# Half-size products in both MLP matmuls, with the gated result through DRAM

## The chip, the cores and the metric

The kernel runs on one core of a Trainium2 chip. The metric is the device time of one execution in microseconds (us). The core has five engines with a queue of their own each: TensorE (PE in the rows; PEld is its weight load), VectorE (DVE), ScalarE (ACT), GpSimd (POOL) and SyncE (SP), which issues all transfers (DMA) here. An engine takes its instructions strictly in the order of its queue and waits at each until its operands are there.

## The reference

Two layers of an encoder, S = 1024 rows, width 1024, in float32. A layer is four groups of attention heads on a common input projection, an output projection and a gated MLP. The change touches the MLP:

```python
        x = x + mix @ w_out[l]

        h = _rmsnorm(x, norm2_g[l])
        u = _dwconv3(h @ w_up[l], conv_w[l], conv_b[l])
        gate, val = u[..., :D_FF], u[..., D_FF:]
        x = x + (jax.nn.silu(gate) * val) @ w_down[l]
```

D_FF is 2816, so w_up is 1024 x 5632 and w_down 2816 x 1024. `_dwconv3` is a convolution of width 3 along the rows, for each column by itself, with a bias.

## The kernel before

A matmul in float32 is made of three in a faster type: `split` stores an operand as a high part (a copy into float32r by ScalarE) and a low part (the operand minus the high part, by VectorE or GpSimd, L130), and `mm` (L141) is called for the three pairs in `PASSES`, high with high and high with low both ways. Each call has a 128x128 weight and 512 moving columns in the MLP.

After attention the second norm turns x, in 8 tiles of 128 rows, into `h2T`, transposed and split: `h2T0` has rows 0 to 511 of the sequence, `h2T1` rows 512 to 1023. This is the tail of the attention stage (`out`, `norm`); its casts of `mT` (the transposed attention result, L1067) and `h2T` (L171) run on ScalarE, the matmuls are `od`, the transposes `ntp`. Its order is written out by hand; the generator `mlp` is advanced inside it and yields after each of its first steps.

The MLP goes over j = 0 to 21 (NFF = 22), 128 of the 2816 columns at a time. `up(j)` loads two 512 KB weights `rawu` (gate part, then value part), splits them (`wu`, high by ScalarE, low by GpSimd), and makes two products `u` of 128 x 1024 in PSUM, 8 chunks of the inner 1024 by 3 passes by 2 halves = 48 matmuls each. `conv` reads u from PSUM (L937 on ScalarE, L938 and L939 on VectorE) and writes `c` in SBUF; `gate` applies silu (L944), multiplies on GpSimd (L945) and splits the result into `gt`. `down(j-1)` then multiplies the previous `gt` with 128 rows of w_down (`rawd`, `wd`): 8 row tiles by 3 passes by 2 halves = 48 matmuls `d`, and VectorE adds each 128 x 1024 result to `xacc`, the running x (L968). So up(j) and down(j-1) alternate, and only down(21) stands alone. j = 0 begins already in the tail of the norm, with the half h2T0. A scheduler places the instructions of the MLP in the queues by its own estimate of when they can run. The pool `raw` has two buffers, `wu`, `wd`, `gt`, `u` and `d` two each.

The order of SP around the start of the MLP matters below: the four small, scattered loads `cw` (conv weights and bias, L917 and L918) are issued ahead of the weights of j = 1 (L922).

## Time and profile before

| | |
|---|---|
| median of 3 runs | 3197.47 us (3197.13 to 3202.42) |
| the profiled execution | 3201.03 us, its span 3199.2 us |
| TensorE busy | 3031.2 us, 95% of the span, 16800 matmuls |
| VectorE, ScalarE, GpSimd busy | 2021.4, 1424.2, 920.5 us (63%, 45%, 29%) |
| granted TensorE clock, mean | 0.987 of full speed |
| MLP of layer 0, from the first u to the last d | 867 to 1605 us |
| MLP of layer 1 | to the end of the span |

The profile is one execution. A row of a group names line, engine, operation and tiles, then the busy time, the mean of one in ns, the idle time of the engine before it and what ended that. A row of a stretch gives for each engine its busy time in that stretch and the count of its instructions. The granted clock is 1.00 at the higher of the two levels (2.4 GHz) and 0.50 at the lower (1.2 GHz).

### The profile page before, as it was taken

The page shows a single profiled execution, that of the slowest core. Times are in us where ns is not written, and L with a number is a line of the kernel's source. Part 1 is how long each engine was busy: PE and PEld are TensorE (multiplying, and loading weights), DVE is VectorE, ACT ScalarE, POOL GpSimd, SP SyncE. Part 2 cuts the span into 40 slices and gives each one's busy share as a digit, 9 for nine tenths or more (in the row PEclk, how much of TensorE's full clock was granted, in tenths as well). Part 3 has the DMA queues.
Part 4 walks back from the last instruction along what each step waited for, and adds up shares of the span by engine and source line. Part 5 has one row for each costly group of instructions (what it writes and reads, how often), then busy time and mean ns, then how long its engine had stood idle before and what let it go on. Part 6 is the DMA issues. An engine that isn't in the chain of part 4 may idle for free. (4 is left out here: it accounts for less than half of the span.)

```text
span 3199.2 us, 44078 instructions
## 1 busy us (share of the span) xinstructions
PE 3031.2 (95%) x16800; PEld 2601.1 (81%) x16800; DVE 2021.4 (63%) x3304; ACT 1424.2 (45%) x2653; POOL 920.5 (29%) x780
## 2 busy tenths in 40 slices
PE   7988899899999999999989899998999999999999
PEld 5978888788888888888769788887888888888887
DVE  6778877777734444444576788777776444444445
ACT  5557765766622222222144577657665222222211
POOL 2265310320232323323222663103201333232221
PEclk9999999999999999999999899999999999999999
DMA  4342241321311111111133322414212111111111
GB/s 140 113 105 67 63 132 40 85 71 31 49 60 46 47 47 47 52 47 50 37 126 108 101 65 66 132 40 91 65 36 39 60 47 53 47 53 40 53 47 66
DMA packets 276867, 212.99 MB, mean 67 GB/s; under 512 B 197168, under 2 KB 242608, under 8 KB 276656
## 3 DMA queue, kind: packets, MB, share of 16 engines
q1 hardware_dynamic: 276656, 210.18, 22.4%
q8 instruction: 132, 2.16, 0.3%
q14 instruction: 79, 0.65, 0.1%
HBM read 157.70 MB, written 41.94 MB: 62 GB/s over the span
## 5 line engine op out<-in xcount | busy, mean ns | idle before, releaser
L141 PE MATMUL u<-h2T,wu 128*128 128x512 f32 x4224 | 1013.7, 392 | 0.0
L141 PEld LDWEIGHTS u<-h2T,wu 128*128 128x128 f32 x4224 | 792.3, 188 | 179.9
L968 DVE TENSOR_TENSOR xacc<-xacc,d 128x1024 f32<-128x1024 f32 x352 | 424.7, 1217 | 460.0 <-PE d L141 459.6
L141 PE MATMUL d<-wd,gt 128*128 128x512 f32 x2112 | 525.7, 392 | 4.1 <-DVE xacc L968 4.1
L141 PE MATMUL pj<-w,hT 128*128 128x256 f32 (+2 forms) x3072 | 494.1, 315 | 24.3 <-ACT w L134 12.9
L141 PEld LDWEIGHTS pj<-w,hT 128*128 128x128 f32 x3072 | 443.0, 196 | 51.5 <-ACT w L134 14.3
L141 PEld LDWEIGHTS d<-wd,gt 128*128 128x128 f32 x2112 | 394.7, 188 | 97.0 <-DVE xacc L968 10.6
L130 POOL TENSOR_TENSOR wu<-rawu,wu 128x1024 fp32r<-128x1024 f32 x88 | 212.3, 2414 | 655.9 <-ACT wu L134 655.9
L487 ACT CAST PT<-pt 128x512 fp32r<-128x512 f32 x448 | 261.6, 584 | 183.7 <-PE pt L145 175.4
L937 ACT ACTIVATE c<-u,cw 128x1024 f32<-128x1024 f32 x88 | 106.3, 1208 | 527.9 <-PE u L141 527.8
L488 DVE TENSOR_TENSOR PT<-pt,PT 128x512 fp32r<-128x512 f32 x448 | 305.1, 686 | 49.6 <-ACT PT L487 47.0
L145 PE MATMUL pt<-cst,P 128*128 128x128 f32 x1792 | 278.5, 279 | 55.2 <-DVE PT L488 49.4
L938 DVE SCALAR_TENSOR_TENSOR c<-u,cw,c 128x1023 f32<-128x1023 f32 x88 | 112.9, 1283 | 297.1 <-ACT c L937 297.0
L145 PEld LDWEIGHTS pt<-cst,P 128*128 128x128 f32 x1792 | 209.7, 142 | 88.7 <-issue 37.8
L141 PEld LDWEIGHTS ot<-PT,v 128*128 128x128 f32 x1664 | 255.7, 192 | 32.1
L141 PE MATMUL ot<-PT,v 128*128 128x256 f32 x1664 | 270.9, 285 | 0.0
L141 PE MATMUL S<-k,q 96*128 96x512 f32 (+2 forms) x512 | 209.6, 435 | 16.9 <-DVE nmb L653 14.9
L141 PE MATMUL od<-wo,mT 128*128 128x512 f32 x768 | 199.9, 399 | 0.9 <-DVE mT L1017 0.7
L130 POOL TENSOR_TENSOR wd<-rawd,wd 128x1024 fp32r<-128x1024 f32 x44 | 105.5, 2398 | 289.4 <-ACT wd L134 289.4
L653 DVE CUSTOM_DVE_ANT_0 P<-S,toep 128x1024 f32<-128x1024 f32 x128 | 155.6, 1219 | 27.3 <-PE pt L145 23.2
L134 ACT CAST gt<-c 128x1024 fp32r<-128x1024 f32 x44 | 46.3, 1053 | 283.5 <-POOL c L945 283.5
L545 DVE TENSOR_REDUCE nm<-S 128x1 f32<-128x1024 f32 x128 | 156.0, 1219 | 19.2 <-PE S L141 18.6
(200 smaller groups left out, 3898.0 us busy)
## 6 DMA issues: line engine op xcount, KB each, us to landing
rawu<-in_w_up_dram SPq DMA_DIRECT2D x88, 512.0 KB, 3.2
rawd<-in_w_down_dram SPq DMA_DIRECT2D x44, 512.0 KB, 3.2
rawi<-in_w_in_dram SPq DMA_DIRECT2D x20, 512.0 KB, 4.0
rawo<-in_w_out_dram SPq DMA_DIRECT2D x16, 512.0 KB, 3.3
sC<-cqk SPq DMA_DIRECT2D x16, 384.0 KB, 2.5
ld<-sB SPq DMA_DIRECT2D x24, 256.0 KB, 3.6
sD<-pe SPq DMA_DIRECT2D x48, 128.0 KB, 1.7
ld<-sC SPq DMA_DIRECT2D x16, 384.0 KB, 3.5
```

What stands on the lines that cost most here:

```text
L130: eng.tensor_tensor(dst[1], src, dst[0].bitcast(F32), op=ALU.subtract)
L134: self.nc.scalar.copy(dst, src)
L141: self.nc.tensor.matmul(out, l, r, start=start, stop=stop)
L145: self.nc.tensor.transpose(out, in_, self.ident[:p, :p])
L487: nc.scalar.copy(PT[:, 0, :], pt)
L488: nc.vector.tensor_tensor(PT[:, 1, :], pt, PT[:, 0, :].bitcast(F32), op=ALU.subtract)
L545: nc.vector.tensor_reduce(nm, Ps["S", i], axis=AX.X, op=ALU.max, negate=True)
L653: nc.vector.tensor_tensor_reduce(out=P, in0=Ps["S", i, s], in1=self.toep[:, o:o + S], scale=-slope, scalar=-NEG, op0=ALU.add, op1=ALU.min, ...
L937: nc.scalar.activation(c, u, AF.Identity, scale=cw[:, 1, jj:jj + 1], bias=cw[:, 3, jj:jj + 1])
L938: nc.vector.scalar_tensor_tensor(c[:, 1:], u[:, :S - 1], cw[:, 0, jj:jj + 1], c[:, 1:], op0=ALU.mult, op1=ALU.add)
L968: nc.vector.tensor_tensor(xacc[:, t, :], xacc[:, t, :], d, op=ALU.add)
```

## The change

Both products are cut two by two (rows and columns of each operand in halves), and the four quarters of the result come from seven half-size products instead of eight, with sums and differences of quarters made beforehand.

In the up product, for j = 1 to 21 (j = 0 stays as it was), the left quarters are the halves of the inner 1024 of gate weight and value weight, `a11`, `a12`, `a21`, `a22`, four sums of which are built in place in the raw buffers by GpSimd (`G`) and VectorE (`V`). The right operands `T1`, `T2`, `T3`, `T4` are built once a layer from `h2T`, which means joining high and low part, four differences and a new split. `T3` overwrites a quarter of h2T1. Each of the seven products has 4 chunks x 3 passes = 12 matmuls into a PSUM tile `X` (8 buffers), and ScalarE, VectorE and GpSimd combine them into `u`, which now lies in SBUF, as `conv` then reads it. The gated result `v` is stored in a DRAM tensor `gd` (11.5 MB per layer) instead of being split.

The down product is a stage of its own after the last gate: `down` loads all 22 tiles of `gd` back (`gg`, 512 KB each) and then runs seven products, each over 11 chunks, where chunk c joins rows c and c + 11 of the 22. A chunk loads one or two 256 KB pieces of w_down (`rawd`, 6 buffers `rw`), adds two of them on GpSimd where two terms are listed in `DOWN`, adds g terms on VectorE, splits both, and issues 4 x 3 = 12 matmuls. The low part of w_down is made by GpSimd for odd c and by VectorE for even c. VectorE adds each finished product to one to two quarters of `xacc`.

The pools move too: `mp` stands on the other side of SBUF, the pool of the attention's output stage is closed earlier and a new one (`oq`) is opened with the last w_out loads, so that these loads and those of j = 0's weights come earlier. `wu` is now cut in halves of the inner dimension, with six buffers.

```diff
@@ -908,10 +908,13 @@
-    def mlp(self, l, xacc, h2T, mp):
+    def mlp(self, l, h2T, mp, gd):
...
         def load(jj):
             raw = self.raw.tile([128, KC, 128], F32, tag="raw", name="rawu")
             nc.sync.dma_start(raw, a["w_up"][l, jj])
-            w = mp.tile([128, 2, KC, 128], F32R, tag="wu", name="wu", bufs=2)
-            self.split((w[:, 0], w[:, 1]), raw, "act", "pool")
-            return w
-
-        def product(u, w, halves):
+            return raw
+
+        def operand():
+            return mp.tile([128, 2, 4, 128], F32R, tag="wu", name="wu", bufs=6)
+
...
+        def gate(j, us):
+            g, v = (conv(jj, u) for jj, u in zip((j, NFF + j), us))
+            nc.scalar.activation(g, g, AF.Silu)
+            G.tensor_tensor(v, v, g, op=ALU.mult)
+            nc.sync.dma_start(gd[j * 128:(j + 1) * 128, :], v)
+
+
+        ws = []
+        for jj in (0, NFF):
+            raw, w = load(jj), []
+            for h in range(2):
+                w.append(operand())
+                self.split((w[h][:, 0], w[h][:, 1]), raw[:, 4 * h:4 * h + 4, :], "act", "pool")
+            ws.append(w)
+        yield
...
-        def gate(us, gt):
-            g, v = us
-            nc.scalar.activation(g, g, AF.Silu)
-            nc.gpsimd.tensor_tensor(v, v, g, op=ALU.mult)
-            self.split((gt[:, 0], gt[:, 1]), v, "act", "dve")
...
-        def down(j, gt):
-            raw = self.raw.tile([128, DM], F32, tag="raw", name="rawd")
-            nc.sync.dma_start(raw, a["w_down"][l, j * 128:(j + 1) * 128, :])
-            w = mp.tile([128, 2, DM], F32R, tag="wd", name="wd", bufs=2)
-            self.split((w[:, 0], w[:, 1]), raw, "act", "pool")
-            for t in range(NT):
-                d = pm.tile([128, DM], F32, tag="d", name="d", bufs=2)
-                for i, (x, y) in enumerate(PASSES):
-                    for n in range(2):
-                        self.mm(d[:, n * 512:(n + 1) * 512], gt[:, x, t * 128:(t + 1) * 128],
-                                w[:, y, n * 512:(n + 1) * 512], i == 0, i == 2)
-                nc.vector.tensor_tensor(xacc[:, t, :], xacc[:, t, :], d, op=ALU.add)
-
...
-            down(j - 1, prev)
+            product(u, w, 1)
+        gate(0, uu)
+        tp, pm = yield
+        T1, T2, T4 = (tp.tile([128, 2, 4, 512], F32R, tag=f"T{i}", name=f"T{i}") for i in (1, 2, 4))
+        T3 = h2T[1][:, :, 0:4, :]
+        B11, B21, B22 = h2T[0][:, :, 0:4, :], h2T[0][:, :, 4:8, :], h2T[1][:, :, 4:8, :]
+
+        for k in range(4):
+            f = [mp.tile([128, 2, 512], F32, tag="u", name="bf", bufs=3) for _ in range(2)]
+            b11, b12, b22, b21 = f[0][:, 0], f[0][:, 1], f[1][:, 0], f[1][:, 1]
+            for d, t in ((b11, B11), (b12, T3), (b22, B22), (b21, B21)):
+                V.tensor_tensor(d, t[:, 0, k, :].bitcast(F32), t[:, 1, k, :].bitcast(F32), op=ALU.add)
+            V.tensor_tensor(b11, b12, b11, op=ALU.subtract)
+            G.tensor_tensor(b12, b22, b12, op=ALU.subtract)
+            V.tensor_tensor(b22, b22, b11, op=ALU.subtract)
+            G.tensor_tensor(b21, b21, b22, op=ALU.subtract)
+            for t, d, eng in ((T1, b11, "dve"), (T2, b22, "dve"), (T3, b12, "pool"), (T4, b21, "pool")):
+                self.split((t[:, 0, k, :], t[:, 1, k, :]), d, "act", eng)
...
+        def prod(w, t):
+            ps = pm.tile([128, 512], F32, tag="X", name="X", bufs=8)
+            i = 0
+            for k in range(4):
+                for x, y in PASSES:
+                    self.mm(ps, w[:, x, k, :], t[:, y, k, :], i == 0, i == 11)
+                    i += 1
+            return ps
+
+        for j in range(1, NFF):
+            rg, rv = load(j), load(NFF + j)
...
+            w11 = op(a11, "pool")
+            G.tensor_tensor(a21, a21, a22, op=ALU.add)
+            s1 = op(a21, "dve")
+            V.tensor_tensor(a11, a21, a11, op=ALU.subtract)
+            s2 = op(a11, "dve")
+            w12 = op(a12, "pool")
+            w22 = op(a22, "pool")
+            G.tensor_tensor(a22, a22, a11, op=ALU.subtract)
+            s3 = op(a22, "pool")
+            V.tensor_tensor(a12, a12, a11, op=ALU.subtract)
+            s4 = op(a12, "dve")
+
...
+            nc.scalar.copy(g[:, lo], prod(w11, B11))
+            nc.scalar.copy(t5, prod(s1, T1))
+            V.tensor_tensor(t2, g[:, lo], prod(s2, T2), op=ALU.add)
+            G.tensor_tensor(g[:, hi], t2, t5, op=ALU.add)
+            V.tensor_tensor(g[:, lo], g[:, lo], prod(w12, B21), op=ALU.add)
+            V.tensor_tensor(v[:, hi], t2, prod(s3, T3), op=ALU.add)
+            V.tensor_tensor(g[:, hi], g[:, hi], prod(s4, B22), op=ALU.add)
+            V.tensor_tensor(v[:, lo], v[:, hi], prod(w22, T4), op=ALU.add)
+            G.tensor_tensor(v[:, hi], v[:, hi], t5, op=ALU.add)
+            gate(j, (g, v))
...
+    DOWN = (
+        (((0, 0, 1),), ((0, 1, 1), (1, 1, -1)), ((0, 1, 1), (1, 1, 1))),
+        (((0, 0, 1), (0, 1, 1)), ((1, 1, 1),), ((0, 0, -1), (0, 1, 1))),
...
+    def down(self, l, xacc, gp, sp, pm, gd):
...
+        for j in range(NFF):
+            gs.append(gp.tile([128, S], F32, tag=f"g{j}", name="gg"))
+            nc.sync.dma_start(gs[-1], gd[j * 128:(j + 1) * 128, :])
+
+        def operand(tag, terms, add, low):
+            w = sp.tile([128, 2, 512], F32R, tag=tag, name=tag, bufs=3)
+            t = terms[0][0]
+            if len(terms) > 1:
+                u, sign = terms[1]
+                d = sp.tile([128, 512], F32, tag="sum", name="sum", bufs=3) if tag == "ga" else t
+                add.tensor_tensor(d, t, u, op=ALU.add if sign > 0 else ALU.subtract)
+                t = d
+            self.split((w[:, 0], w[:, 1]), t, "act", low)
+            return w
+        for As, Bs, Cs in self.DOWN:
+            ds = [pm.tile([128, 512], F32, tag="d", name="d", bufs=8) for _ in range(4)]
+            for c in range(NH):
+                ta = [(gs[c + NH * k][:, i * 512:(i + 1) * 512], sign) for i, k, sign in As]
+                tb = []
+                for k, j, sign in Bs:
+                    raw = sp.tile([128, 512], F32, tag="rw", name="rawd", bufs=6)
+                    r0 = (c + NH * k) * 128
+                    nc.sync.dma_start(raw, a["w_down"][l, r0:r0 + 128, j * 512:(j + 1) * 512])
+                    tb.append((raw, sign))
+                w = operand("ga", ta, V, "dve")
+                m = operand("wd", tb, P, "pool" if c % 2 else "dve")
+                for t in range(4):
+                    for i, (x, y) in enumerate(PASSES):
+                        self.mm(ds[t], w[:, x, t * 128:(t + 1) * 128], m[:, y, :], c == 0 and i == 0, c == NH - 1 and i == 2)
+            for i, j, sign in Cs:
+                for t in range(4):
+                    xs = xacc[:, 4 * i + t, j * 512:(j + 1) * 512]
+                    V.tensor_tensor(xs, xs, ds[t], op=ALU.add if sign > 0 else ALU.subtract)
...
-                    st["mlp"] = self.mlp(l, st["x"], h2, me.enter_context(self.pool(f"mp{l}", side=gs)))
+                    st["mlp"] = self.mlp(l, h2, me.enter_context(self.pool(f"mp{l}", side=at)), gd)
...
-            try:
-                st["mlp"].send(me.enter_context(self.pool(f"pm{l}", space=PS)))
-            except StopIteration:
-                pass
+            o2.close()
+            with ExitStack() as te:
+                try:
+                    st["mlp"].send((te.enter_context(self.pool(f"T{l}", side=gs)), te.enter_context(self.pool(f"pm{l}", space=PS))))
...
             halves.close()
-            oe.close()
+            with ExitStack() as te:
+                self.down(l, xacc, te.enter_context(self.pool(f"G{l}", side=gs)), te.enter_context(self.pool(f"dw{l}", side=gs)),
+                          te.enter_context(self.pool(f"pd{l}", space=PS)), gd)
```

ScalarE in the tail of layer 0's second norm, before the change. `rawu_9862` and `rawu_9867` are the weights of j = 0:

```order
L134 CAST wu_9864<-rawu_9862 128x1024
L134 CAST wu_9869<-rawu_9867 128x1024
L1067 CAST mT_9877<-mtp_9872 128x256
L171 CAST h2T0_8975<-ntp_9885 128x4x128
L155 ACTIVATE od2_9830,nss_9844<-xacc_4940 128x1024
L171 CAST h2T0_8975<-ntp_9892 128x4x128
L1067 CAST mT_9880<-mtp_9872 128x256
L1067 CAST mT_9923<-mtp_9918 128x256
```

Only j = 0's weights are cast here. The same place on ScalarE after the change (`rawu_9867` and `rawu_9875` belong to j = 0, `rawu_10290` to j = 1):

```order
L134 CAST wu_9877<-rawu_9875 128x512
L134 CAST wu_9880<-rawu_9875 128x512
L1159 CAST mT_9888<-mtp_9883 128x256
L171 CAST h2T0_9311<-ntp_9896 128x4x128
L155 ACTIVATE od2_9835,nss_9849<-xacc_4941 128x1024
L171 CAST h2T0_9311<-ntp_9903 128x4x128
L1159 CAST mT_9891<-mtp_9883 128x256
L134 CAST wu_10294<-rawu_10290 128x512
L1159 CAST mT_9934<-mtp_9929 128x256
L171 CAST h2T0_9311<-ntp_9942 128x4x128
```

A cast of j = 1's gate weight now stands between two casts of mT, ahead of the rest of the norm.

SP at the end of layer 0's MLP, before; `rawq` and `rawk` are weights of the next layer:

```order
L959 DMA rawd<-in_w_down_dram 128x1024
L922 DMA rawu<-in_w_up_dram 128x1024 x2
L959 DMA rawd<-in_w_down_dram 128x1024
L922 DMA rawu<-in_w_up_dram 128x1024 x2
L959 DMA rawd<-in_w_down_dram 128x1024 x2
L1149 DMA rawq<-in_c_wqb_dram 128x2x384
L1153 DMA rawk<-in_c_wkvb_dram 128x512
```

Loads of both weights alternate up to the end. SP at the end of the up product of layer 0, after the change:

```order
L925 DMA rawu<-in_w_up_dram 128x1024 x2
L942 DMA gd_1774<-c 128x1024
L925 DMA rawu<-in_w_up_dram 128x1024 x2
L942 DMA gd_1774<-c 128x1024
L1241 DMA rawq<-in_c_wqb_dram 128x2x384
L1245 DMA rawk<-in_c_wkvb_dram 128x512
L942 DMA gd_1774<-c 128x1024 x2
L1049 DMA gg<-gd_1774 128x1024 x22
L1069 DMA rawd<-in_w_down_dram 128x512 x106
```

The w_down loads, which alternated with the w_up loads, now all stand behind the last two stores of gated results and the 22 loads of g.

GpSimd in the middle of the MLP, for one j, before:

```order
L945 TENSOR_TENSOR c<-c 128x1024
L130 TENSOR_TENSOR wu<-rawu,wu 128x1024
L130 TENSOR_TENSOR wd<-rawd,wd 128x1024
L130 TENSOR_TENSOR wu<-rawu,wu 128x1024
L945 TENSOR_TENSOR c<-c 128x1024
```

That is a product and three splits for one j. GpSimd for one j of the up product, after the change (`t_11041` and `t_11042` are the tiles t2 and t5):

```order
L1021 TENSOR_TENSOR u<-t_11041,t_11042 128x512
L130 TENSOR_TENSOR wu<-rawu,wu 128x512 x2
L1010 TENSOR_TENSOR rawu<-rawu 128x512
L130 TENSOR_TENSOR wu<-rawu,wu 128x512
L1026 TENSOR_TENSOR u<-u,t_11042 128x512
L1004 TENSOR_TENSOR rawu<-rawu 128x512
L130 TENSOR_TENSOR wu<-rawu,wu 128x512
L941 TENSOR_TENSOR c<-c 128x1024
```

Three splits and a product of 128x1024 became eight instructions on 128x512 and the product, and the last two of the eight (L1004 and L130 ahead of L941) belong to a later j.

## Rows read from the trace of the kernel before

**Rows 1.** the page: busy us and share; TensorE's granted clock in 40 slices.

```profile
PE 3031.2 (95%) x16800; PEld 2601.1 (81%) x16800; DVE 2021.4 (63%) x3304; ACT 1424.2 (45%) x2653; POOL 920.5 (29%) x780
...
PEclk9999999999999999999999899999999999999999
```

**Rows 2.** a stretch: busy us by engine (PE, PEld, DVE, ACT, POOL); clock, DMA, GB/s.

```profile
915.00:1580.00 665.00, 665.00 (x2883) 541.12 (x2882) 309.88 (x260) 148.75 (x140) 189.99 (x79) 1.00 0.14 47
```

**Rows 3.** costliest groups of the page, the two MLP products: busy us, mean ns.

```profile
L141 PE MATMUL u<-h2T,wu 128*128 128x512 f32 x4224 | 1013.7, 392 | 0.0
...
L141 PE MATMUL d<-wd,gt 128*128 128x512 f32 x2112 | 525.7, 392 | 4.1 <-DVE xacc L968 4.1
```

**Rows 4.** the stretch at the end of layer 0, columns as in rows 2.

```profile
1583.00:1606.00 23.00, 21.20 (x84) 14.96 (x84) 19.63 (x18) 2.87 (x4) 2.39 (x1) 1.00 0.34 140
```

**Rows 5.** timeline of TensorE between the layers: start, us, instruction, [idle before it].

```profile
1612.05 1.30 PE L145 MATMUL ntp<-cst,nx 128*128 128x128 f32 x5 [6.69 <-DVE nr L117]
```

**Rows 6.** timeline of SP (issues) in the tail of layer 0's second norm.

```profile
849.43 8.01 SPq L917 DMA_DIRECT2D cw<-in_conv_w_dram  x3
857.48 3.31 SPq L918 DMA_DIRECT2D cw<-in_conv_b_dram  x1
860.83 3.63 SPq L922 DMA_DIRECT2D rawu<-in_w_up_dram  x1
```

**Rows 7.** tile rawu, 855 to 870 us: time from issue to landing.

```profile
DMA to landing us min/median/max: 5.1/6.4/7.6
```

**Rows 8.** timeline of ScalarE in the tail of the norm.

```profile
853.69 0.38 ACT L1067 CAST mT<-mtp 128x256 fp32r<-128x256 f32 x1
```

**Rows 9.** tile wo, its splits: ns min/median/max, first and last start, shape.

```profile
L130 POOL TENSOR_TENSOR wo<-rawo,wo x32: 720/747/931, 412.7 to 2395.3; 128x256 fp32r<-128x256 f32 x32
L130 DVE TENSOR_TENSOR wo<-rawo,wo x32: 407/620/969, 413.6 to 2397.0; 128x256 fp32r<-128x256 f32 x32
```

**Rows 10.** line 968, one operand in PSUM, columns as in rows 9.

```profile
L968 DVE TENSOR_TENSOR xacc<-xacc,d x352: 1208/1220/1222, 917.2 to 3194.4; 128x1024 f32<-128x1024 f32 x176
```

**Rows 11.** groups of GpSimd by shape: busy us, mean ns, idle before.

```profile
L130 POOL TENSOR_TENSOR wu<-rawu,wu 128x1024 fp32r<-128x1024 f32 x88 | 212.3, 2414 | 655.9 <-ACT wu L134 655.9
...
L945 POOL TENSOR_TENSOR c<-c 128x1024 f32<-128x1024 f32 x44 | 105.5, 2397 | 73.0 <-DVE c L939 71.6 <-issue 1.4
...
L130 POOL TENSOR_TENSOR w<-rawi,w 128x512 fp32r<-128x512 f32 x32 | 40.7, 1290 | 1.3 <-ACT w L134 1.1
```

**Rows 12.** groups of VectorE by shape, columns as in rows 11.

```profile
L938 DVE SCALAR_TENSOR_TENSOR c<-u,cw,c 128x1023 f32<-128x1023 f32 x88 | 112.9, 1283 | 297.1 <-ACT c L937 297.0
...
L130 DVE TENSOR_TENSOR gt<-c,gt 128x1024 fp32r<-128x1024 f32 x44 | 53.7, 1220 | 13.3 <-ACT gt L134 13.3
...
L130 DVE TENSOR_TENSOR w<-raw,w 128x512 fp32r<-128x512 f32 x16 | 10.7, 688 | 4.3 <-ACT w L134 4.3
```

**Rows 13.** timelines of GpSimd and VectorE in the third wo split.

```profile
712.25 3.18 POOL L130 TENSOR_TENSOR wo<-rawo,wo 128x256 fp32r<-128x256 f32 x4 [6.68 <-ACT wo L134]
...
713.05 1.79 DVE L130 TENSOR_TENSOR wo<-rawo,wo 128x256 fp32r<-128x256 f32 x2
```

**Rows 14.** DMA issues over the whole span: KB each, us to landing.

```profile
rawu<-in_w_up_dram SPq DMA_DIRECT2D x88, 512.0 KB, 3.2
...
ld<-sB SPq DMA_DIRECT2D x24, 256.0 KB, 3.6
...
mx<-mix SPq DMA_DIRECT2D x22, 256.0 KB, 2.6
```

**Rows 15.** groups of ScalarE by shape, columns as in rows 11.

```profile
L937 ACT ACTIVATE c<-u,cw 128x1024 f32<-128x1024 f32 x88 | 106.3, 1208 | 527.9 <-PE u L141 527.8
...
L944 ACT ACTIVATE c<-c 128x1024 f32<-128x1024 f32 x44 | 46.7, 1062 | 117.3 <-DVE c L939 117.3
```

**Rows 16.** a stretch of layer 1 with many loads, columns as in rows 2.

```profile
2008.00:2022.00 14.00, 10.23 (x43) 8.51 (x43) 9.82 (x19) 6.65 (x13) 1.13 (x2) 0.63 1.02 395
```

**Rows 17.** the restart after the gap between the layers, columns as in rows 2.

```profile
1617.00:1622.00 5.00, 4.89 (x11) 3.48 (x12) 4.67 (x10) 3.44 (x8) 1.34 (x1) 0.50 0.53 169
```

More of the change, by code (lines that the diff above doesn't have):

```diff
@@ L1185, in run @@
             h2, wo = [], []
[L1186 removed]
+            halves, me, o2 = ExitStack(), ExitStack(), ExitStack()
+            gd = dp.tile([FF, S], F32, tag=f"gd{l}", name=f"gd{l}")
             def norm2(t, r):
```

63 lines of the change are left out of this document (31 added, 32 removed), and 5 rows, old and new, of the table DOWN.

## The prediction

> **What bounds the kernel now.** I read the page first, then the engines by stretch, then the places where TensorE waits. TensorE is busy for 95% of the span at full clock in nearly every slice [rows 1]. In the gated MLP it is the only limit: between 915 and 1580 us it is busy for all of 665.00 us and issues 2883 matmuls, so one 128x512 matmul costs 665.00/2883 = 0.2307 us [rows 2], while VectorE works for 47% of that stretch and GpSimd for 29%. The two MLP products hold 4224 and 2112 matmuls [rows 3], 6336 x 0.2307 = 1462 us of the 3201. Fewer matmuls there shorten the kernel one for one, as long as the other engines and the transfers stay beside them. That condition is what has to be examined.
>
> **What the change removes.** Each j from 1 to 21 of the up product takes 7 x 12 = 84 matmuls in place of 96, so 252 fewer per layer. The down product takes 7 x 11 x 12 = 924 in place of 1056, so 132 fewer. 384 x 0.2307 = 88.6 us per layer, **177 us** in all. The last 84 down matmuls of layer 0 begin at 1583 and are done at 1612.05 - 6.69 = 1605.4, 22.4 us against 84 x 0.2307 = 19.4, since there are two accumulators that VectorE must drain [rows 4, 5]; with eight half-size ones that goes: **6 us** in two layers. Between the layers TensorE idles 6.69 us for the next norm [rows 5]; rows 0 to 511 of x are now final before the last product, so I take **5 us** for this. Removed: 188 us, 3201 - 188 = 3013.
>
> **What it adds at the start of the MLP.** In the new order ScalarE casts j=1's first weight between two casts of mT. That weight's DMA stands on SP behind the four cw loads, whose issue takes 8.01 and 3.31 us, so it is issued at 860.83 and lands 5.1 to 7.6 us later [rows 6, 7], at some 868.4. ScalarE would come there at 854.1, just after the cast of 853.69 [rows 8]; it waits 14 us, and the norm of the second half, the transposes and the first u products all queue behind it. With a restart at half clock I take **16.5 us** a layer (8 to 20), 33 in all.
>
> **What VectorE and GpSimd do to each other.** The change puts many 128x512 sums and differences of two SBUF operands on both. Where they meet in the trace they exclude one another: in the wo split a GpSimd 128x256 takes 720 ns alone and up to 931, a VectorE one 407 alone and up to 969 [rows 9]. VectorE's xacc adds, which have one operand in PSUM, stay at 1208 to 1222 ns in all 352 cases, whatever GpSimd does [rows 10]. The price of a turn: from 512 to 1024 columns GpSimd grows by 2.414 - 1.290 = 1.124 us and VectorE by 1.220 - 0.688 = 0.532 [rows 11, 12]; these parts cannot overlap. Four GpSimd and two VectorE rows of 256 columns stand in 3.18 us [rows 13]: 4 x 0.562 + 2 x 0.266 = 2.78, the rest is 0.067 a turn. So a 128x512 turn costs 1.19 on GpSimd and 0.60 on VectorE. No row shows so dense a mixture for long; the sum of turns is my value, the two ends are no exclusion at all and full durations.
>
> The Trainium skill states the rule ("SBUF — State Buffer", Who interferes with whom): a VectorE instruction with two SBUF inputs and a GpSimd one that reads SBUF exclude each other, and the loser is blocked for the whole instruction. The trace agrees that they do, but 3.18 us for that group is less than 4 x 0.720 + 2 x 0.407 = 3.69, so whole durations are too dear by its rows.
>
> - *The T operands*, once a layer: 32 VectorE turns and 16 GpSimd turns, 32 x 0.60 + 16 x 1.19 = 38.2 us, with the first gate's product (2.3) and what is left of j=1's operands (4) 44.5 us after the second half of h2T. The cover is 48 u0 matmuls (11.1) and the seven products of j=1 (19.4), 30.5 us. Lost: 14, and as the first sums read h2T0 alone I take **13** a layer, 26 in all. Without exclusion VectorE alone needs 32 x 0.688 and j=0's four conv rows at 1.28, 27 us, and the last T come some 5 late; by full durations 32 x 0.688 + 16 x 1.29 + 2.4 + 4.5 = 49.5, 19 late [rows 11, 12].
> - *The up product in its steady state.* Per j, GpSimd has eight 128x512 and one 128x1024 (10 x 1.124 + 9 x 0.067 = 11.84 us). VectorE has five 128x512 and four conv rows of 128x1023, whose u now lies in SBUF (13 x 0.532 + 9 x 0.067 = 7.52). Together 19.36, against 84 x 0.2307 = 19.38 on TensorE: exactly level. Operands are made about 8 us before they are needed and eight PSUM tiles hold the results, so single collisions are hidden; but any moment in which neither has work (the casts between, the raw load of 3.2 us for the next j [rows 14]) is then late. I take 0.4 us per j, 42 x 0.4 = **17 us**. Ends: 0, and by full durations 8 x 1.29 + 2.40 + 5 x 0.688 + 4 x 1.28 = 21.28, so 1.9 per j, 80 us [rows 11, 12].
> - *The down product.* Two chunks are 24 matmuls, 5.54 us. Three of the seven products have two terms on both sides: GpSimd 3 turns (3.57), VectorE 5 (3.0), 6.57 us, over by 1.03 on 16.5 pairs of chunks. Two products have two w_down terms and one g term; their turns sum to 5.37, but a loop stands there: GpSimd's low part frees a buffer, SP loads 256 KB into it, GpSimd adds (1.29) and makes the next low part (1.29), one such round for two chunks. A 256 KB transfer lands after 2.6 to 3.6 us [rows 14]; 2.6 + 0.1 + 2.58 with one VectorE turn of 0.6 between is 5.9, over by 0.4 on 11 pairs. 16.5 x 1.03 + 11 x 0.4 = 21.4 a layer, **43 us**. Ends: 5 (landing 2.6, no collision) and 88 (full durations, landing 3.6).
>
> **What it adds between the products.** Formerly down(j-1) ran beside up(j), now it begins when the last gate is done. After the last up matmul: VectorE's add 0.69 and conv 1.28, ScalarE's silu 1.06 and conv 1.21, VectorE 2 x 1.28, GpSimd's product 2.40 [rows 11, 12, 15], about 10 us with the semaphores. SP issues the stores of j=20 and 21, then 22 loads of g, and only then w_down, in that order on one queue. With all DMA engines busy the core moves 395 GB/s [rows 16], so 512 KB take 1.33 us; 25 such portions are 33 us, and with some 2 us of latency the first pair of w_down lands 45 us after the last up matmul. Sum and split are another 2 us, and TensorE restarts at half clock, as it ran for 1617 to 1622 after the gap between the layers [rows 17]: 2.5 us. **49 us** a layer, 98 in all (90 to 110). Nothing covers it, since TensorE has no other work there. The rest (the stores of g, smaller and more w_down loads, four late adds at the very end) lies beside other work; its cover is a DMA share of 0.14 [rows 2].
>
> **The sum.** 3013 + 33 + 26 + 17 + 43 + 98 = 3230 us for the profiled execution. The profiled run of before, 3201.0, is 3.6 us over its median of 3197.5, so the forecast is **3226 us**, 0.9% slower: the transitions (157 us) and the shared path (60) eat the 188.
>
> **Rivals.** (1) *Faster:* VectorE and GpSimd are kept apart by their queues. For: in the old MLP they hardly meet, and the operands' lead is 8 us. Against: 19.36 of 19.38 us leaves nothing to place. Then T loses 5 a layer, up 0, down 5: 3013 + 33 + 10 + 5 + 98 = 3159, median 3155. It decides once the three terms, 86 in my sum, fall under 57. (2) *Much faster:* the gap between the products is also short, because transfers of g overlap or the first w_down pair overtakes them. At 20 us a gap instead of 49 this takes 58 more off, about 3100. Against: the one queue. (3) *Clearly slower:* each of the two engines holds the other off for its whole instruction: 38 for T, 80 for up, 88 for down, 3013 + 33 + 38 + 80 + 88 + 98 = 3350, median 3346. Against: the 3.18 us group. It decides once a turn costs its whole duration. (This is what the Trainium skill's section named above gives for this kernel.) (4) *No change:* terms between mine and rival 1 that meet the 188.
>
> **How the numbers follow.** Forecast, 3204 to 3280: 0.47. Rival 1, 3110 to 3191: 0.25. Rival 2: 0.05. Rival 3, 3280 to 3350: 0.13. Rival 4, within 0.2% (about what a measurement of this kernel can tell from no change): 0.10. Faster 0.30, same 0.10, slower 0.60. The range 3115 to 3305 leaves out the lower part of rivals 1 and 2 and the upper half of rival 3.
>
> **What would show it.** In the new profile: u and d matmuls per layer down by 384; a ScalarE wait of some 14 us for rawu before the second half of the norm; a TensorE gap of 45 us or more between the last X and the first d matmul, filled with DMA at full share; VectorE's 128x512 rows of two SBUF operands well over 0.69 us on average while xacc stays at its price; TensorE's idle before d charged to GpSimd or VectorE. The prediction is wrong if VectorE's rows keep 0.69 in the down stage, if that gap is under 35 us, or if one j of the up stage takes more than 20.5 us.

## The result, and the profile after

The changed kernel takes 3306.28 us (median of 4 runs, 3300.18 to 3312.43) against 3199.94 us beside it (median of 4, 3197.13 to 3205.09). The ratio is 1.033, with a 95% interval of 1.0304 to 1.0357: it is slower, in the direction of the forecast, but by 3.3% instead of 0.9%. The forecast was 3226 us with a range of 3115 to 3305; the time lies just above the range. The profiled execution has a span of 3301.1 us, 101.9 more than before.

The page, to be set beside [rows 1]: busy us, share of the span, count; below it TensorE's clock in 40 slices.

```profile
PE 2896.7 (88%) x16032; PEld 2458.4 (74%) x16032; DVE 2526.5 (77%) x3836; ACT 1646.8 (50%) x3203; POOL 1488.4 (45%) x1204
...
PEclk9999999999989999889999899999999999997999
```

768 matmuls are gone, as planned, and TensorE is busy for 135 us less. The span nevertheless grew: it now stands idle for 12% of it instead of 5%. The costliest groups say where. Columns: busy us, mean ns of one, then the idle time of the engine before them and what ended it; these answer [rows 3, 11, 12].

```profile
L141 PE MATMUL X<-h2T,wu 128*128 128x512 f32 x2016 | 498.7, 397 | 67.8 <-POOL wu L130 66.3
L141 PE MATMUL d<-wd,ga 128*128 128x512 f32 x1848 | 436.3, 395 | 122.2 <-ACT wd L134 100.3
...
L130 POOL TENSOR_TENSOR wu<-rawu,wu 128x512 fp32r<-128x512 f32 x176 | 261.6, 1498 | 92.9 <-ACT wu L134 92.9
...
L130 DVE TENSOR_TENSOR wu<-rawu,wu 128x512 fp32r<-128x512 f32 x126 | 161.0, 1278 | 71.4 <-ACT wu L134 66.0
```

Two idle times are new: 66.3 us before matmuls of the up product, ended by GpSimd's low parts, and 100.3 us before the down product, which are the two gaps between the products. The last two rows show VectorE and GpSimd holding each other off: a 128x512 low part on VectorE, 688 ns before [rows 12], takes 1278 on the mean, and one on GpSimd 1498 instead of 1290 [rows 11].

The same stage by stage, from the starts of the matmuls in the trace (us, layer 0 and layer 1; the loss is against matmuls of 0.2307 us without a pause):

| | measured | lost | forecast |
|---|---|---|---|
| from the start of the tail to the first u (layer 1: with the boundary ahead of it) | 13.2 and 18.5 later | 32 | 33 - 5 |
| j = 1, with the T operands beside it | 36.4, 34.2 | 32 | 26 |
| j = 2 to 21 | 430.6, 427.8 | 83 | 17 |
| gap between the last X and the first d | 50.0, 50.3 | 100 | 98 |
| down product | 229.3, 229.0 | 32 | 43 |
| 768 matmuls less | | -177 | -177 |

The losses sum to 279, and 279 - 177 = 102 is the 101.9 measured (two small things cancel: waits inside the old MLP that are gone, such as the drain, and a span that ends 2 us later after the last matmul). One term stands out: the up product's steady state.

Its rows are these. From the waits of TensorE in layer 0's up product (us in total, times, longest):

```profile
PE X L141 <- POOL wu L130: 33.7, 34, 2.0
PE X L141 <- ACT T L134: 7.5, 2, 7.0
PE X L141 <- DVE T L130: 4.4, 2, 3.6
```

and one j on GpSimd, VectorE and SP, from their timelines (start us, us, instruction, [idle before it and what ended it]):

```profile
1305.95 1.30 POOL L1004 TENSOR_TENSOR rawu<-rawu 128x512 f32<-128x512 f32 x1 [4.39 <-DMA rawu<-in_w_up_dram]
1307.21 1.31 POOL L130 TENSOR_TENSOR wu<-rawu,wu 128x512 fp32r<-128x512 f32 x1
1308.45 2.87 POOL L941 TENSOR_TENSOR c<-c 128x1024 f32<-128x1024 f32 x1
```

```profile
1300.32 1.78 DVE L130 TENSOR_TENSOR wu<-rawu,wu 128x512 fp32r<-128x512 f32 x1
...
1307.94 1.12 DVE L130 TENSOR_TENSOR wu<-rawu,wu 128x512 fp32r<-128x512 f32 x1 [1.54 <-ACT wu L134]
1308.98 2.89 DVE L1006 TENSOR_TENSOR rawu<-rawu 128x512 f32<-128x512 f32 x1
...
1319.68 0.68 DVE L1025 TENSOR_TENSOR u<-u,X 128x512 f32<-128x512 f32 x1
1320.28 1.71 DVE L935 SCALAR_TENSOR_TENSOR c<-u,cw,c 128x1023 f32<-128x1023 f32 x1
1321.91 1.78 DVE L130 TENSOR_TENSOR wu<-rawu,wu 128x512 fp32r<-128x512 f32 x1
```

```profile
1299.34 3.12 SPq L925 DMA_DIRECT2D rawu<-in_w_up_dram  x2
...
1320.93 3.12 SPq L925 DMA_DIRECT2D rawu<-in_w_up_dram  x2
```

The order to read them in: at 1300.32 VectorE makes the low part of s4, the last reader of the gate weight's buffer, until 1302.1. Only then can the next load into that buffer leave; GpSimd, with nothing else to do for 4.39 us, gets it at 1305.95. Sum, cast, low part follow, and then L1006, which stands behind GpSimd's gate product (1308.45 to 1311.32) and takes 2.89 us instead of 0.69. The chain runs on through the other operands to the next low part of s4, at 1321.91, which also had to wait on VectorE's queue behind a conv row of the j before. From low part to low part are 21.59 us, and 21.6 is what a j takes. So a load of 3.9 us (1302.1 to 1305.95) and 17.7 us of turns stand in one loop, one after the other.

### The profile page after: what moved, and what is told of

It reads as the page before. It is cut to its first block, busy times and chain, and to the rows that moved or that the text cites. A ratio compares the mean times of both kernels' runs of the same rounds, so it can differ in the third digit from the quotient of the medians.

```text
span 3301.1 us, 45354 instructions
## 1 busy us (share of the span) xinstructions
PE 2896.7 (88%) x16032; PEld 2458.4 (74%) x16032; DVE 2526.5 (77%) x3836; ACT 1646.8 (50%) x3203; POOL 1488.4 (45%) x1204
## 5 line engine op out<-in xcount | busy, mean ns | idle before, releaser
L141 PE MATMUL X<-h2T,wu 128*128 128x512 f32 x2016 | 498.7, 397 | 67.8 <-POOL wu L130 66.3
L141 PE MATMUL d<-wd,ga 128*128 128x512 f32 x1848 | 436.3, 395 | 122.2 <-ACT wd L134 100.3
L141 PEld LDWEIGHTS X<-h2T,wu 128*128 128x128 f32 x2016 | 370.5, 188 | 181.7 <-POOL wu L130 96.7
L141 PE MATMUL pj<-w,hT 128*128 128x256 f32 (+2 forms) x3072 | 487.4, 312 | 20.5 <-ACT w L134 10.9
L141 PEld LDWEIGHTS d<-wd,ga 128*128 128x128 f32 x1848 | 346.9, 190 | 211.6 <-ACT wd L134 101.1
L141 PEld LDWEIGHTS pj<-w,hT 128*128 128x128 f32 x3072 | 438.2, 194 | 45.5 <-ACT w L134 11.9
L141 PE MATMUL X<-T,wu 128*128 128x512 f32 x1512 | 368.9, 396 | 23.4 <-ACT T L134 14.5
L141 PEld LDWEIGHTS X<-T,wu 128*128 128x128 f32 x1512 | 286.9, 190 | 91.2 <-ACT T L134 17.0
L488 DVE TENSOR_TENSOR PT<-pt,PT 128x512 fp32r<-128x512 f32 x448 | 304.7, 684 | 47.7 <-ACT PT L487 45.4
L134 ACT CAST wu<-rawu 128x512 fp32r<-128x512 f32 x302 | 174.5, 617 | 316.8 <-DVE rawu L1006 157.5
L130 POOL TENSOR_TENSOR wu<-rawu,wu 128x512 fp32r<-128x512 f32 x176 | 261.6, 1498 | 92.9 <-ACT wu L134 92.9
L145 PEld LDWEIGHTS pt<-cst,P 128*128 128x128 f32 x1792 | 210.5, 143 | 83.6 <-issue 34.2
L1057 POOL TENSOR_TENSOR rawd<-rawd 128x512 f32<-128x512 f32 x110 | 167.4, 1523 | 162.9 <-DMA rawd<-in_w_down_dram 148.5
L141 PE MATMUL S<-k,q 96*128 96x512 f32 (+2 forms) x512 | 211.6, 439 | 20.6 <-DVE nmb L653 17.7
L130 DVE TENSOR_TENSOR wu<-rawu,wu 128x512 fp32r<-128x512 f32 x126 | 161.0, 1278 | 71.4 <-ACT wu L134 66.0
```

The source lines that it names most:

```text
L130: eng.tensor_tensor(dst[1], src, dst[0].bitcast(F32), op=ALU.subtract)
L134: self.nc.scalar.copy(dst, src)
L141: self.nc.tensor.matmul(out, l, r, start=start, stop=stop)
L145: self.nc.tensor.transpose(out, in_, self.ident[:p, :p])
L488: nc.vector.tensor_tensor(PT[:, 1, :], pt, PT[:, 0, :].bitcast(F32), op=ALU.subtract)
L1057: add.tensor_tensor(d, t, u, op=ALU.add if sign > 0 else ALU.subtract)
```

## The experiments

In the expectations theory A is this reading: two raw buffers, each held until its last low part, put the load and the turns into one loop, and either one taken out brings a j down. Against it stands that the blocked rows alone, without the load, cost the 2.2 us. "After" is the changed kernel, whose j takes 21.3 to 23 us once the first few have passed. The runs were made on several chips, on which the kernel before took 3199.9 to 3208.3 us, and among kernels with the same tail the first u of layer 0 came between 878.6 and 889.2 us. So the readings go by stages, and a difference of a few us between two whole times says little.

**e1_quarters: the raw buffers cut in four.** The same 8 KB per partition, but each quarter is loaded by itself, into the slot that came free first.

```diff
-            rg, rv = load(j), load(NFF + j)
-            a11, a12, a21, a22 = rg[:, 0:4, :], rg[:, 4:8, :], rv[:, 0:4, :], rv[:, 4:8, :]
+            a21, a22, a11, a12 = slots
+            slots = [a21, a11, a22, a12]
+            for q, jj, h in ((a21, NFF + j, 0), (a22, NFF + j, 1), (a11, j, 0), (a12, j, 1)):
+                nc.sync.dma_start(q, a["w_up"][l, jj][:, 4 * h:4 * h + 4, :])
```

> Each j's up weights are loaded as four quarters of 256 KB, each into the place that the quarter used earliest leaves free, in the same 8 KB; nothing else is edited. Theory A (the next j's raw load stands in series in a loop with the turns of VectorE and GpSimd, since both raw buffers are held until the last low part): with the load off the loop one j of the up product takes 19.4 to 20.0 us in place of 21.6, and the kernel about 65 us less, 3235 to 3250. Theory B (the turns themselves fill 21.6 us): one j stays at 21 us or more and the kernel within 15 us of 3306.

Measured: 3243.0 us, 63 less than after; j = 2 to 21 give 72 us of it, and the first u of layer 0 came 8.7 us later. A j takes 19.24 us from the second to the tenth in layer 0, without any loss, and 19.9 from there on. GpSimd's 4 us waits for rawu are gone from its waits (1000 to 1320 us of the span):

```profile
POOL wu L130 <- ACT wu L134: 34.6, 30, 1.3
POOL c L941 <- DVE c L935: 18.6, 16, 1.2
```

Theory A holds for the larger part: without the load in the loop 2.2 us a j become 0.5 to 0.7. VectorE's rows did not become faster; L1010 (the former L1006) still takes 2.5 us, so blocked rows alone cost at most that remainder.

**e2_one_sbuf_input and e2c_six_X: the other end, turns taken away.** In e2 every VectorE row of the up product with two SBUF operands gets a constant in PSUM in place of the second one (the computation is thereby incomplete, in the operands and the conv). The constant takes two of eight banks, so `X` has six buffers; e2c has the six buffers and the unused constant alone.

```diff
-            ps = pm.tile([128, 512], F32, tag="X", name="X", bufs=8)
+            ps = pm.tile([128, 512], F32, tag="X", name="X", bufs=6)
...
+        Z = pm.tile([128, S], F32, tag="Z", name="Z", bufs=1)
+        V.memset(Z, 0.0)
...
-            V.tensor_tensor(a11, a21, a11, op=ALU.subtract)
+            sub(a11, a21)
```

> In the up product's j = 1 to 21 each of VectorE's nine rows that had two whole SBUF operands now takes its second whole operand from a constant PSUM tile (the right one is still named as a scalar, so that the waits stay), which leaves the sums, low parts and convolutions wrong; X has six PSUM buffers instead of eight. The loads are as in the changed kernel. Theory A (mutual exclusion of two-operand VectorE rows and GpSimd lengthens the loop by some 5 us): VectorE's 128x512 rows fall to 0.69 us, GpSimd's to 1.29, and one j to 19.4 to 19.8, about 75 us less in all. Theory C (the loop is long by the load and the casts, the exclusion is hidden): the rows get shorter but one j stays over 20.8 us.

> Only the control for the run with one SBUF input: the constant PSUM tile is there and unused, X has six buffers instead of eight. Both theories: one j at 21.4 to 22.0 us and the kernel at 3300 to 3320; if it is clearly slower, six buffers cost by themselves.

Measured: e2 3521.44 us, 24.6 to 27.9 a j; e2c 3301.63, like after, with 21.3 a j. In e2 the rows fell as they should (tile rawu, ns min/median/max):

```profile
L1005 DVE SCALAR_TENSOR_TENSOR rawu<-rawu,Z x24: 739/745/749, 1014.9 to 1311.1; 128x512 f32<-128x512 f32 x24
L1023 POOL TENSOR_TENSOR rawu<-rawu x12: 1271/1288/1303, 1019.6 to 1312.3; 128x512 f32<-128x512 f32 x12
```

but the scheduler, for which these are other instructions, put the making of all operands of a j into one block behind its conv rows, and TensorE waits for that block ("PE X <- DVE wu", 59.8 us in 320). The run shows that the exclusion hangs on the second SBUF operand. On the loop it says nothing, since the order changed with it.

**e2d_conv: the conv rows alone.** This edit keeps the order. Only the four conv rows of a j read the constant (their accumulation is left out); otherwise as e2c.

```diff
-            V.scalar_tensor_tensor(c[:, 1:], u[:, :S - 1], cw[:, 0, jj:jj + 1], c[:, 1:], op0=ALU.mult, op1=ALU.add)
+            V.scalar_tensor_tensor(c[:, 1:], u[:, :S - 1], cw[:, 0, jj:jj + 1], c[:, 1:] if Z is None else Z[:, 1:], op0=ALU.mult, op1=ALU.add)
```

> The changed kernel with its own loads, only that the four convolution rows of VectorE per j add a constant PSUM tile instead of c (this makes the convolution wrong), six X buffers; the order of VectorE and GpSimd stays that of the changed kernel. Theory A (load and turns stand in one loop): GpSimd's rows next to the convolutions lose about 1 us of waiting, the last low part about 0.4, and one j falls from 21.3 (the control with six buffers) to 20.0 to 20.6. Rival (the loop is the load alone): one j stays within 0.3 us of 21.3.

Measured: 3256.46 us; most js take 20.2 to 20.9, against 21.3 in e2c. Fewer turns shorten the loop, but the load keeps it above 20 us: GpSimd still waits for it.

```profile
POOL rawu L1006 <- DMA rawu<-in_w_up_dram: 72.3, 15, 5.2
```

**e7_quarters_conv: both.** The edits of e1 and e2d together (the conv is incomplete here too).

> The quarter loads of the earlier run, and besides in j = 1 to 21 the four convolution rows of VectorE per j add a constant PSUM tile instead of c, so that they have one SBUF operand (this makes the convolution wrong); six X buffers. With quarter loads one j takes 19.93 us after the first ten, 0.7 over TensorE's 19.24. Theory A (that remainder is the turns on the shared path, 19.36 us and a little idleness): four turns of some 1.13 us go, and all 21 j run at 19.2 to 19.3, 20 to 25 us less than 3243. Rival (the remainder is the chain of casts and loads): one j stays at 19.8 to 20.

Measured: 3207.27 us, and every j but the first at 19.24 in layer 0 and 19.16 in layer 1. So the 0.7 us that e1 left were turns on the shared path, and with that the 83 us are accounted for: the load in the loop, and the rest turns. The kernel is 36 us under e1, where 20 to 25 were expected: j = 2 to 21 give 17.6 of them, and the rest lies outside, with 8.6 in the two gaps (45.7 and 45.4 us).

**e3_lazy_g: the gap.** The gap of 50 us was forecast from one SP queue: 22 loads of g ahead of the first w_down. Here each g is loaded where it is first used.

```diff
-        for j in range(NFF):
-            gs.append(gp.tile([128, S], F32, tag=f"g{j}", name="gg"))
-            nc.sync.dma_start(gs[-1], gd[j * 128:(j + 1) * 128, :])
...
+                for j in {c + NH * k for _, k, _ in As}:
+                    if gs[j] is None:
+                        fetch(j)
```

> The tiles of g are loaded where a chunk first names them, so that the first w_down pair is issued behind one load of g and not behind 22. Theory D (the gap of 50 us is one queue in order at some 400 GB/s): the gap between the last X and the first d falls to 17 to 22 us, the first of the seven products becomes bound by loads (22 x 512 KB and 22 x 256 KB at 1.3 us per 512 KB, 43 us in place of 34), the kernel 40 to 50 us less, about 3260. Theory E (the gap is the round trip of store and load through DRAM): it stays over 40 us.

Measured: 3295.15 us. The gap falls from 50.0 to 23.6 us. Timeline of TensorE, after first, then e3:

```profile
1423.12 3.35 PE L141 MATMUL d<-wd,ga 128*128 128x512 f32 x7 [49.99 <-ACT wd L134]
```

```profile
1403.46 9.91 PE L141 MATMUL d<-wd,ga 128*128 128x512 f32 x36 [23.55 <-ACT wd L134]
```

But the first down product takes 51.6 us instead of 34.1. On SP the scheduler set the g loads of later products between and ahead of this product's w_down loads, up to five in a row (SP's timeline of e3):

```profile
1417.56 0.33 SPq L1073 DMA_DIRECT2D rawd<-in_w_down_dram  x1
1418.17 1.60 SPq L1050 DMA_DIRECT2D gg<-gd  x2
1420.78 0.33 SPq L1073 DMA_DIRECT2D rawd<-in_w_down_dram  x1
1422.03 4.21 SPq L1050 DMA_DIRECT2D gg<-gd  x5
```

The gap is the queue, as forecast, though it stayed a little above the 17 to 22 us expected. Of the 26 us that it lost, 17.5 were only moved, and the kernel is 11 us under after instead of 40 to 50.

**e4_cw_early_rw12: the tail, and the down stage's buffers.** The four cw loads are issued right behind j = 0's weights, where nobody waits behind them; and `rw` has twelve buffers instead of six.

```diff
+        with self.tc.issue_after(load.ins.ins):
+            for i in range(3):
+                nc.sync.dma_start(cw[:, i, :], a["conv_w"][l, i].rearrange("(j p) -> p j", p=128))
...
-                    raw = sp.tile([128, 512], F32, tag="rw", name="rawd", bufs=6)
+                    raw = sp.tile([128, 512], F32, tag="rw", name="rawd", bufs=12)
```

> Two edits that act in different stages. The conv weights cw are loaded right behind the first up weights, into a tile of the constants, instead of in the tail of the norm: theory A (ScalarE waits for a weight that stands behind cw on SP) has the first u matmul back at 867 to 870 us in layer 0 in place of 880, and some 13 us less in layer 1. And the w_down loads have twelve buffers instead of six: if the down product is bound by its load loop, all seven products come to 30.4 to 31.5 us; if by turns of VectorE and GpSimd, those with one g term (31.4 to 32.3) come to 30.5 to 31, those with two terms on both sides stay at 33 to 35.5. The kernel: 3268 to 3282 by the second, 3245 by the first.

Measured: 3285.1 us. The first u of layer 0 comes at 868.1 us (after 880.1, before 866.9), and layer 1's comes 857.6 us after the end of layer 0's MLP (after 874.7, before 856.2). The wait that this takes away is the one ScalarE had in after, as read ahead from [rows 6 to 8]; the same cast in after, then in e4:

```profile
866.24 0.62 ACT L134 CAST wu<-rawu 128x512 fp32r<-128x512 f32 x1 [14.15 <-DMA rawu<-in_w_up_dram]
```

```profile
854.07 0.62 ACT L134 CAST wu<-rawu 128x512 fp32r<-128x512 f32 x1 [1.93 <-DMA rawu<-in_w_up_dram]
```

The twelve buffers gave nothing: the down product takes 232.5 and 235.9 us instead of 229. They do let the loads run further ahead. When the third product begins, 44 pieces of w_down have been issued in after and 54 in e4 (issues up to there, after first):

```profile
rawd<-in_w_down_dram SPq DMA_DIRECT2D x44, 256.0 KB, 2.9
```

```profile
rawd<-in_w_down_dram SPq DMA_DIRECT2D x54, 256.0 KB, 3.2
```

From the third product of layer 0 on, a piece lands 27 to 32 us before the first matmul of its chunk (mean of each product), in after 10 to 14. SP's waits in the third product are nearly the same all the same, first after, then e4:

```profile
SPq L1069 <- POOL rawd L1057: 12.8, 10, 1.8
SPq L1069 <- POOL wd L130: 4.1, 4, 1.4
```

```profile
SPq L1070 <- POOL rawd L1058: 13.6, 10, 1.5
SPq L1070 <- POOL wd L130: 5.8, 5, 1.3
```

Loads wait for GpSimd's sum of w_down terms (L1057, in e4 L1058) with six buffers as with twelve, and the sum waits for its loads; with twelve buffers this merely happens for later chunks. GpSimd works in the order of its queue, and there the sum of a later chunk stands ahead of the low part that TensorE needs next. In e4 the sum for the first chunk of the fourth product waits 1.86 us for its load, and behind it stands the low part for the fourth chunk of the third product, whose first matmul starts at 1487.06 us:

```profile
1484.81 1.40 POOL L1058 TENSOR_TENSOR rawd<-rawd 128x512 f32<-128x512 f32 x1 [1.86 <-DMA rawd<-in_w_down_dram]
1486.17 1.74 POOL L130 TENSOR_TENSOR wd<-rawd,wd 128x512 fp32r<-128x512 f32 x1
```

So the loop that the prediction closed over the low part closes mostly over the sum, and loads that land early do not lift it. No run changed the order of sum and low part, so that this order is what costs the time is read from the trace and not tested.

**e9_no_g_sums, e10_no_w_sums, e11_w_sums_8_columns: turns or loop in the down product.** e9 leaves out VectorE's sums of g, e10 GpSimd's sums of w_down; e11 keeps the latter with their waits, but over 8 of 512 columns.

```diff
-            if len(terms) > 1:
+            if len(terms) > 1 and tag != "ga":
```

```diff
-            if len(terms) > 1:
+            if len(terms) > 1 and tag != "wd":
```

```diff
+                n = 512 if tag == "ga" else 8
+                add.tensor_tensor(d[:, :n], t[:, :n], u[:, :n], op=ALU.add if sign > 0 else ALU.subtract)
```

> Leaves out the sums of g terms that VectorE makes in the down stage (the first term alone is used); the sums of w_down terms stay. Turns: for the three products with two terms on both sides VectorE has 3 turns in place of 5 in two chunks, 3.57 + 1.8 = 5.37 us against 5.54 on TensorE, so products 4, 5 and 7 of a layer go from 33 to 35.6 us to 30.5 to 31.2; products 1 and 3 (one g term) stay at 34 and 31.5 to 32.3. Rival (each product ends with 4 to 8 adds to xacc that hold VectorE's splits): nothing changes, 33 to 35.6.

> Leaves out the sums of w_down terms that GpSimd makes in the down stage (both pieces are still loaded, the first alone is used); VectorE's sums of g stay. Turns: 1.19 + 5 x 0.60 = 4.2 us against 5.54 in two chunks, so all products but the first at 30.4 to 30.7 us, the first at 32.5 with its start at half clock: 214 to 216 us a layer from the first d to the last instead of 229. Rival (adds to xacc at the ends of products): products 4, 5 and 7 stay at 33 to 35.6.

> As after, but the sum of two w_down terms covers 8 of the 512 columns, so that it stays in its place with its waits and frees its buffer as before, at nearly no length (the rest of the first term is used unsummed: part of the computation is left out). Turns: 1.19 + 5 x 0.60 = 4.2 us against 5.54 in two chunks, so every product but the first at 29.9 to 30.7 us, the fifth too, which took 36.7 and 39.3 where the sums were dropped altogether and the second load lost its reader. If the load loop (landing 2.8, cast, low part) is the limit in itself, the fifth stays at 34 to 39.

Measured, the seven products of layer 0 in us (132 matmuls without a pause are 30.5):

| | 1 | 2 | 3 | 4 | 5 | 6 | 7 | sum |
|---|---|---|---|---|---|---|---|---|
| after | 34.1 | 30.4 | 31.4 | 33.0 | 35.6 | 30.4 | 34.2 | 229.3 |
| e9 | 33.9 | 29.9 | 31.5 | 34.6 | 34.1 | 29.9 | 31.2 | 225.1 |
| e10 | 31.5 | 30.4 | 29.9 | 30.4 | 36.7 | 32.2 | 32.1 | 223.2 |
| e11 | 32.2 | 30.4 | 33.2 | 35.1 | 36.4 | 30.4 | 31.6 | 229.3 |

None of the three did all that the turns alone would give, though single products did (e9's seventh, e10's third and fourth). In e11 GpSimd's sums are short (0.37 us on the mean) and VectorE's low parts of g are back at 0.72 us in the fifth product, yet products 3 to 5 are no faster. GpSimd's waits there, in the fourth product:

```profile
POOL rawd L1058 <- DMA rawd<-in_w_down_dram: 23.2, 9, 3.8
```

It waits for a load in 9 of 11 chunks, with the low parts behind it in its queue, and SP's next load waits in turn, first for an earlier load and then for the sum (15.7 and 5.0 us there). In e10, where that step is gone, the first, third and fourth products run without a loss beyond the start; in the fifth TensorE is late again, while SP's loads wait for earlier loads (25.5 of 37 us), as they do in the third (21.0 of 30) without harm: in the third a piece still lands 10.8 us before the first matmul of its chunk on the mean, in the fifth 0.6 us. e11 rules out that the length of GpSimd's sum is the limit, and together with e10 it points to the place of the sum, after its loads and ahead of the low parts. What sets the 33 to 36 us of the fourth and fifth products stays open.

**e6_all and e8_all_conv_psum: the parts put together.** e6 has e1's quarters, e4's early cw and twelve buffers, e3's late g loads with SP's order in the down stage kept as written, and the two products that use the same g first.

```diff
+                with tc.manual_schedule(engines={mybir.EngineType.SP}):
+                    self.down(l, xacc, *pools, gd)
...
-        for As, Bs, Cs in self.DOWN:
+        for As, Bs, Cs in (self.DOWN[i] for i in (0, 6, 1, 2, 3, 4, 5)):
```

> Quarter loads, early cw, twelve w_down buffers, and SP's order in the down stage as written: per chunk one load of g (only where the chunk needs it) and its w_down pieces; the product that again needs the first half of g comes second. From the single runs: up 63 us less, tails 26 less, gap 50 to 20-24 us twice, 55 less, the first product up to 2 us longer: 3150 to 3175, below the kernel before (3200). Rival (the gap is the round trip through DRAM): the gap stays over 40 and the kernel over 3195.

Measured: 3160.41 us against 3205.37 beside it, ratio 0.986 (0.9843 to 0.9877). It is faster than after and, by 1.4%, than before. The gap is 23.2 us and the first product after it 34.7, so what e3 lost again is kept here; a j is 19.04 us, later 19.87.

e8 adds what e7 showed, with the conv kept whole: c stands in PSUM until its last row, and X has six buffers. `rw` has six buffers again. The products keep e6's order: the expectation has them in their first order, but the edit did not put them back.

```diff
-            c = mp.tile([128, S], F32, tag="c", name="c", bufs=3)
+            c = d = mp.tile([128, S], F32, tag="c", name="c", bufs=3)
+            if pm is not None:
+                c = pm.tile([128, S], F32, tag="Z", name="cp", bufs=1)
...
-            V.scalar_tensor_tensor(c[:, :S - 1], u[:, 1:], cw[:, 2, jj:jj + 1], c[:, :S - 1], op0=ALU.mult, op1=ALU.add)
+            V.scalar_tensor_tensor(d[:, :S - 1], u[:, 1:], cw[:, 2, jj:jj + 1], c[:, :S - 1], op0=ALU.mult, op1=ALU.add)
+            if pm is not None:
+                nc.scalar.copy(d[:, S - 1:], c[:, S - 1:])
```

> The kernel of e6_all with three changes: the conv of j = 1 to 21 is kept in a PSUM tile between its steps (so that its four VectorE rows have one SBUF input; six X tiles instead of eight), the w_down buffers are six again, and the products of the down stage stand in their first order. It computes everything. Theory A (what is left in a j of e6_all, 19.87 us, is turns of the four conv rows): every j at 19.04 to 19.25 us, 24 us less in two layers. The buffers: down products as in e6_all within 1 us each, so 3160 - 24 = 3136 us. Rival (the 19.87 is a loop of buffers, X above all): j at 19.9 or more, 3160 or slower. Rival on the buffers (six raw buffers slow the down products): 3145 to 3160 with j at 19.1.

Measured: 3119.41 us (median of 4 runs, 3115.69 to 3124.99) against 3205.18, ratio 0.974 (0.9718 to 0.9762), the fastest of all. Each j from 2 to 20 takes 19.04 us, and between 1000 and 1320 us TensorE has no wait at all. The conv rows are at the price of [rows 12] in all cases of that stretch; in e6 the second of each pair was held (tile c, ns min/median/max, e6 and then e8):

```profile
L932 DVE SCALAR_TENSOR_TENSOR c<-u,cw,c x32: 1715/1959/2201, 1004.9 to 1309.0; 128x1023 f32<-128x1023 f32 x32
```

```profile
L934 DVE SCALAR_TENSOR_TENSOR c<-u,cw,cp x34: 1272/1278/1281, 1000.1 to 1317.7; 128x1023 f32<-128x1023 f32 x34
```

The gain over e6 is 41 us, more than the 24 expected. The js give 10 us of it per layer, which is most of the 24, and the gap 4 (it is 19.0 us). Most of the rest is that the first u comes earlier, in layer 0 at 871.5 us instead of 877.0; that lies ahead of what was edited, and the first u moves by that much between runs with the same tail, so no cause in e8 is shown for it. The down product is as slow as ever, 232.0 and 229.7 us against 233.0 and 230.1 in e6: in the same order of products, six buffers do as well as twelve.

## Why the prediction was right in sign and wrong in size

**The step that failed** is the steady state of the up product: "any moment in which neither has work (the casts between, the raw load of 3.2 us for the next j) is then late. I take 0.4 us per j", 17 us. It measured 83 us, 2.1 for each of the 40 j from 2 to 21, beyond even the upper end of 80. The exclusion itself was priced well: with the load out of the loop (e1) a j settles at 19.9 us, near the 19.36 of the sum of turns and far from the 21.28 of whole durations. What was missing is the loop. The prediction named the raw load as a moment without work and then let the lead of 8 us cover most of it. But a lead can only build up if the next load can leave early, and there are two raw buffers, each held until the last low part made from it, the second until the end of the j's turns. The load then adds to the turns in full: 3.9 + 17.7 us, against 19.38 on TensorE. The prediction drew exactly such a loop for the down product, with buffer, load, sum and low part, and did not draw it for the up product, which has two buffers where the other has six. It gave 20.5 us for one j as the point beyond which it would be wrong, and that is where it was. Replacing 17 by 83 in its sum gives 3230 + 66 = 3296 us for the profiled execution, which took 3303.

**The bound** of 1.9 per j was whole durations of both engines' rows put end to end, a bound on the turns. As a bound on the j it was none, since the load lay outside it.

**The tail** was right in place and size: ScalarE waits 14.15 us for the rawu behind cw (14 forecast), 13.2 us in layer 0 where 16.5 were taken, and e4 gives back 12.0 us of it, in layer 1 17.1. **The boundary** between the layers was near, by another way than the one named: the wait for the norm did not shrink but grew, 11.0 us in place of 6.69 [rows 5], while a wait of 3.12 us for w right behind it is gone. A hundred projection matmuls (`pj`) into layer 1 the kernel is 2.5 us ahead of the one before, counted from the last d of layer 0, where 5 were taken.

**The T operands** cost 17 and 15 us a layer where 13 were taken, of which 11.9 in layer 0 are the waits for ScalarE's and VectorE's part of T shown above. No run took them apart.

**The gap** was right: 50.0 us against 49, by the queue on SP, which e3 shows. Its parts were each off a little: the first g load left 15 us after the last X, not 10, and from there to the first d were 35 us, not 39.

**The down product** cost 16 us a layer where 21.5 were taken. That the loss would lie in products with two w_down terms held (products 2 and 6, with one, run at 30.4 us), but the split into turns and loop is not borne out by e9 to e11. Nor is the loop of buffer and load the limit as it was drawn: a piece lands 10 to 14 us ahead in after and 27 to 32 in e4, and the products take as long. So that the term came near, 43 against 32 us in two layers, is in part luck.

**The rivals.** Rival 3 came nearest in time, 3346, but by another mechanism than it named. Its rule is the Trainium skill's ("SBUF — State Buffer", Who interferes with whom). The trace agrees with that rule for a single row: L1006 ends 0.55 us after GpSimd's gate product, so it was held for all of the rest of it. What it adds up to over a j is less than the 21.28 us of whole durations, by e1's 19.9 us. What rivals 1 and 2 had in mind, 3155 and 3100 us, is what the change can give once the loop, the tail and the queue are out: e8's 3119.

## What to carry to other kernels

Before saying that an operand's lead hides a step, list for each buffer who reads it last, and draw the loop from that reader through the next load back to it; everything in the loop adds up, and the sum stands against the time of one turn of the bound engine. Two engines that exclude one another lengthen such a loop even while each of them still has idle time. When a stage of its own replaces interleaved work, look first at what stands ahead of its first load on the issuing queue, and after moving that, at where the scheduler puts it next. And before giving a pool more buffers, look whether the engine that takes its tiles has early work for a later chunk ahead of the work that is due: then loads that land early may change nothing, as in e4.

## What the runs showed of the hardware beyond what was expected

A VectorE row is held or free by where its operands lie, not by its operation. In after the 128x512 adds with X in PSUM keep 675 to 680 ns in every group, while L1006, of the same size with two SBUF operands, takes 2.73 us on the mean:

```profile
L1006 DVE TENSOR_TENSOR rawu<-rawu 128x512 f32<-128x512 f32 x42 | 114.5, 2727 | 6.4 <-POOL rawu L1004 3.9 <-POOL wu L130 2.5
...
L1025 DVE TENSOR_TENSOR u<-u,X 128x512 f32<-128x512 f32 x42 | 28.6, 680 | 0.0
```

Moving one operand of the conv rows from SBUF to PSUM (e8) took the second of each pair from 1959 to 1278 ns (medians).

More buffers let loads run ahead and gained nothing: with twelve in place of six a piece of w_down landed 27 to 32 us before its matmuls instead of 10 to 14, and the down product took 232.5 us instead of 229.3.
